# Last stage of a decoder block: the first of seven block products is placed one step forward, and the newest MLP tile's transpose is issued on ScalarE's DMA queue

## The chip, the cores and the metric

The kernel runs on one core of one Trainium2 chip. The metric is device time in microseconds of that core for one execution, as the median of repeated runs. Before the change it is 1565.66 us over three runs (1565.0, 1565.66 and 1566.17).

## The reference

One layer (`DEPTH = 1`) for 256 tokens of width 2048, all in float32. Ahead of the part that matters here come a norm, one wide projection, a sparse attention and a retention branch, their gated sum and a projection `w_out` that is added to `x`. What the change touches is the end of the MLP:

```python
h2 = rms_norm(x, ln2_g[l])
x = x + jnp.square(jax.nn.relu(h2 @ w_ff1[l])) @ w_ff2[l]     # w_ff1 2048 x 8192, w_ff2 8192 x 2048
```

The output is (1, 256, 2048) float32.

## The kernel before

**Products.** A float32 product is made of three TensorE (PE) matmuls. Weights and activations are each split into a rounded part `hi` and a rest `lo`, and `products` (L477 to L479) adds act-hi with weight-hi, act-hi with weight-lo and act-lo with weight-hi into one PSUM bank. ScalarE (ACT) writes a weight tile's `whi` at L427, VectorE (DVE) writes its `wlo` at L429, for 128x1024 elements at a time, from a `raw` tile that SyncE (SP) loads at L382 (1 MB each). `weights(item)` hands out such a pair; it also starts the loads and splits of the items that follow in the list `use`.

**The MLP.** The 8192 hidden columns go in eight groups of 1024 (g = 0 to 7). A group's hidden values are made with tokens on the partitions, as tiles of 128 tokens x 512 columns, named by token half t and column half i. For the second matmul each tile is turned by `turn_in`: ACT gathers the two 16-bit halves of every word into `halves` (L519), a DMA transposes that into the tile itself (L523, 256 KB, on SP's queue), ACT puts the words together again (L528), and `split_into` splits them into `act` hi (ACT, L501) and lo (DVE, L502). L519 writes what the DMA reads, and L528 waits for it to land. In the last group (LAST = 7) the two tiles of i = 1 come first, then (t 0, i 0), and (t 1, i 0) is the newest: its `halves` is the last L519 of the program.

**The last stage.** `ending` multiplies the last group's hidden values with its 1024 rows of `w_ff2`. Its order is written by hand in `ESTEPS`. A step (i, h, s) stands for column block i (512 columns) and two of the eight row tiles, half h and pair s within it; it takes both token halves, so 2 x 2 x 3 = 12 matmuls of 128x512 (in block 3, token half 1 is done in two pieces of 256 columns). For blocks 1 and 2 only the half h = 0 is done so. Their half h = 1 is done by the seven products of a 2 x 2 block scheme: a number n in `ESTEPS` is product n, of 6 matmuls, and `ETILES` and `PRODUCTS` say which weight tile (A to D) and which form of the activations it takes. Products 0 and, later, others use `act` as it is; four forms are differences of quarters of `act` (`fm`, made in `end_forms`, L1470 and L1474 on DVE, split at L506 on ACT and L507 on DVE). Weight tiles are added in place at L413 between products (A + B when step (0, 0, 1) is reached, and so on, by `ESUMS`).

Product 0 takes weight tile A and the form X11, the quarter of `act` with token half 0 and the first two row tiles of half 1, that is hidden tile (t 0, i 1). Step (0, 0, 0) takes row tiles of half 0 in both token halves, that is the hidden tiles (t 0, i 0) and (t 1, i 0).

**What else stands there.** The partial sums of the earlier groups are in DRAM (`sums`); GpSimd (POOL) adds to them by DMA (L1460) what ACT scales at L1459. `stream(i)` reads block i back into `room` (L1494, on SP's queue; block 0 at step (3, 1, 0), block 2 at product 0). ACT copies products 0, 1 and 3 out of PSUM at L1532; DVE combines them (L1534, L1537, L1538), adds them to `room` (L1498), and ACT issues the output DMAs (L1501).

**What sets the order.** Each engine runs its own instructions in a fixed order. `step()` advances every generator in `work` by one `yield`, once an item, so moving an item also moves what the generators and `weights` emit around it. A wait on ACT, on DVE or in SP's queue holds everything behind it on that engine.

Of the kernel before, what the change touches and what calls it, by code (L numbers as in the profile page):

```python
# [13 lines left out]
U16 = mybir.dt.uint16  # L14
# [4 lines left out]
P = 128  # L19
# [110 lines left out]
def merged(g):  # L130

    f = iter([("F2", g - 1, i, h, s) for i, h in F2_COLS for s in range(KC // HC)])
    out = []
    for n, p in enumerate(ORDER):
        for h in range(HK // KC):
            out += [("Q", g, n, h, s) for s in range(KC // HC)]
            out.append(next(f))
        if p == 4:
            out.append(next(f))
    return out + list(f)  # L140
# [9 lines left out]
OTHERS = [(("O", i), h) for i in range(3) for h in range(DK // KC)]  # L150
LAST = NG - 1
ETILES = {"A": (1, 0), "B": (2, 0), "C": (2, 1), "D": (1, 1)}
ESTEPS = ((0, 1, 0), (0, 1, 1), (3, 1, 0), (3, 1, 1), (0, 0, 0), 0, (0, 0, 1), 1, (1, 0, 0), 2, (1, 0, 1), 3, 4, (2, 0, 0), 5, (2, 0, 1), 6,
          (3, 0, 0), (3, 0, 1))
BEHIND = {0: (2, 1), 2: (1, 0), 1: (2, 0), 3: (3, 0)}
STREAMS = {(3, 1, 0): 0, (1, 0, 0): 1, (2, 0, 0): 3}
# [23 lines left out]
def block_kernel(ctx, tc, cst, rot, xt, gains, w, x, ret_gn_g, ret_gn_b, out):  # L180
    nc = tc.nc
# [29 lines left out]
    W_NORM, W_SOFT, W_GN, W_CROSS, W_ROWS, W_LAST, W_QUERY, W_PROBS, W_INDEX = 3, 5, 7, 8, 7, 6, 5, 5, 5  # L211
# [4 lines left out]
    def nm(s):  # L216
        uid[0] += 1
        return f"{s}_{uid[0]}"
# [6 lines left out]
    def mid(shape, dtype=F32):  # L225
        return late["ep"].tile(list(shape), dtype, tag="mid", name=nm("mid"), bufs=n_mid[late["ep"].name])
# [66 lines left out]
    for g in range(1, NG):  # L293
        use += merged(g)
    use += [("F2", LAST) + z if type(z) is tuple else ("E", z, ETILES[PRODUCTS[ORDER[z]][1]][1]) for z in ESTEPS]

# [199 lines left out]
    def split_into(act, k0, nk, t, ps):  # L496

        src = ps.rearrange("p (c i) -> p c i", c=nk)
        hi = act[0][:, k0:k0 + nk, t * P:(t + 1) * P]
        lo = act[1][:, k0:k0 + nk, t * P:(t + 1) * P]  # L500
        nc.scalar.activation(hi, src, AF.Copy)  # L501
        nc.vector.tensor_tensor(lo, src, hi.bitcast(F32), op=ALU.subtract)  # L502
# [6 lines left out]
    def interleaved(a):  # L509
        return a.bitcast(U16).rearrange("p (j h) -> p h j", h=2)  # L510

    def planes(a):
        return a.bitcast(U16).rearrange("p (h j) -> p h j", h=2)

    def turned(src, halves, wait, tied=False, dst=None, mirror=None, gap=1):

        mirror = src if mirror is None else mirror
        with tc.issue_after(late["split"]) if tied else nullcontext():
            nc.scalar.activation(planes(halves), interleaved(src), AF.Copy)  # L519
        for _ in range(gap):  # L520
            yield
        with tc.issue_after(late["loaded"]) if gap > 1 else nullcontext():
            nc.sync.dma_start_transpose(mirror.bitcast(U16).rearrange("p (c r) -> p c r", r=P), halves.bitcast(U16))  # L523
        for _ in range(wait):
            yield
        with tc.issue_after(late["split"]):
            if dst is None or len(dst.shape) == 2:
                nc.scalar.activation(interleaved(halves if dst is None else dst), planes(mirror), AF.Copy)  # L528
            else:
                nc.scalar.activation(dst.bitcast(U16).rearrange("p c (i h) -> p h c i", h=2), planes(mirror).rearrange("p h (c i) -> p h c i", i=P), AF.Copy)  # L530

    def turn_in(act, k0, t, src, tile_for, wait, land=W_CROSS, tied=False, mirror=None, gap=1):

        for _ in range(wait):
            yield
        halves = tile_for((P, BN))
        yield from turned(src, halves, land, tied, mirror=mirror, gap=gap)
        split_into(act, k0, 4, t, halves)

    hT = act_pair(0)  # L540
# [86 lines left out]
    def key_tile(t, a):  # L627

        for _ in range(2 * t):
            yield  # L630
        halves = ep.tile([P, BN], F32, tag="halves", name=nm("halves"), bufs=2)
        yield from turned(a, halves, W_CROSS + 2)
        nc.scalar.activation(kT[:, :, t * P:(t + 1) * P], halves.rearrange("p (h i) -> p h i", h=4), AF.Copy, scale=gqk)
# [6 lines left out]
    def index_tile(t, half):  # L640

        for _ in range(t if half else 4 + 2 * t):
            yield
        if "iqT" not in late:
            late["ik2"] = mid([P, T, 2, ID])
            late["iqT"] = ep.tile([P, IH // 2, S], F32, tag="a1", name="iqT")
        c = IH // 4
        dst = late["iqT"][:, half * c:(half + 1) * c, t * P:(t + 1) * P]
        yield from turned(iqs[:, t, half * BN:(half + 1) * BN], stage(), W_INDEX + t if half else W_CROSS, dst=dst)
        turned_iq.add((t, half))  # L650
# [159 lines left out]
    for j in range(NKV):  # L810
        ps = run_block(("AQ", j), of(hT))
        r = cp.tile([P, GRP * T], F32, name=nm("r"))
# [198 lines left out]
    for gate, u in ((z, u) for z in BESIDE for u in range(2)):  # L1011
# [10 lines left out]
        for item in beside(gate, u):  # L1022
# [10 lines left out]
            else:  # L1033
                branch(item, of(oT if gate == "GA" else hT))
                i = item[0][1] - 2 * u
# [57 lines left out]
    def normed(j, ys, gb, sg):  # L1093
        mv, vr, nb = small(4 * T), small(2 * T), small(2 * T)
        for t in range(T):
            for a in range(2):
                st = small(6)
                nc.vector.bn_stats(st, ys[t][:, a * RV:(a + 1) * RV])
                nc.vector.bn_aggr(mv[:, 4 * t + 2 * a:4 * t + 2 * a + 2], st)
        mean, var = (mv.rearrange("p (a b) -> p a b", b=2)[:, :, i] for i in range(2))  # L1100
        nc.vector.tensor_copy(vr, var)
        yield
        r = rsqrt(vr, 2 * T, 1.0)
        nc.vector.scalar_tensor_tensor(nb, mean, -1.0, r, op0=ALU.mult, op1=ALU.mult)
        yield
        for t in range(T):
            y = ys[t]
            for a in range(2):
                c = slice(a * RV, (a + 1) * RV)
                i = 2 * t + a  # L1110
                nc.scalar.activation(y[:, c], y[:, c], AF.Identity, scale=r[:, i:i + 1], bias=nb[:, i:i + 1])
            nc.vector.tensor_tensor(y, y, gb[0], op=ALU.mult)
            nc.vector.tensor_tensor(y, y, gb[1], op=ALU.add)
            yield
            nc.vector.tensor_tensor(y, y, sg[t], op=ALU.mult)
            work.append(turn_in(rT, 4 * j, t, y, halves, *((W_GN - 1 + t,) if j < 2 else (W_GN - 3 + t, 5))))

    for j in range(4):
        if j < 2:

            i = j
# [5 lines left out]
        for src in (ret_gn_g, ret_gn_b):  # L1127
            g = mid([P, BN])
# [71 lines left out]
    for i in range(4):  # L1200
        ms = mss[i] if i in pair else gates(i)
        ps = run_block(("UR", i), of(rT), ps=pair.get(i), k0=PARTS[-1][0] * KC if i in pair else 0)
        for t, m in enumerate(ms):
            g = sgb[:, t, i * BN:(i + 1) * BN]
            nc.vector.tensor_tensor(g, ps[t], g, op=ALU.mult)
            nc.vector.tensor_tensor(m, m, g, op=ALU.add)
            if i < 2:
                work.append(turn_whole(i, t, m))
            elif i < 3:
                work.append(turn_in(mT, 4 * i, t, m, mid, 2 + 2 * t))  # L1210
            else:
                tails.append(turn_in(mT, 4 * i, t, m, kept, 0, 11, mirror=kept((P, BN)), gap=6))
                next(tails[-1])
# [184 lines left out]
    def put(*new):  # L1398
        for (t, i), z, src in new:
            ys[t, i] = squared(z, src)  # L1400
        for (t, i), _, _ in new:
            hidden(g, t, i)
# [4 lines left out]
    def hidden(g, t, i):  # L1407
        act, y = [z[:, g % 2 * FG:] for z in hid[:2]], ys.pop((t, i))
        wait, room, land = (1 + 2 * t, spread if g or not i else stage, 7 if g or i else 4 + t)
        if g and not i:  # L1410
            wait, land = {NG - 1: ((3, 4), (0, 2))}.get(g, ((4, 9), (1, 8)))[t]
        turn = turn_in(act, 4 * i, t, y, room, wait, land, g > 0)
        work.append(marked(turn, t) if (g, i) == (LAST, 1) else turn)

    def marked(turn, t):
        yield from turn
        inner.append(t)
# [8 lines left out]
    for i, part in F1_PARTS:  # L1426
        up[i] = run_block(("F1", i), lambda k, t: form(blocks[k // HK][t], k % HK), ps=up.get(i),
                          k0=part[0] * KC, k1=(part[-1] + 1) * KC)
        if part[-1] < DK // KC - 1:
            continue  # L1430
        for t in range(T):
            ys[t, i] = squared(stage(), up[i][t])
            if i:
                hidden(0, t, i)
# [145 lines left out]
    for t in range(T):  # L1580
        hidden(0, t, 0)
# [43 lines left out]
```

## Time and profile before

| | |
|---|---|
| median of 3 runs | 1565.66 us (1565.0 to 1566.17) |
| the profiled execution's own time | 1565.19 us |
| its span, first to last instruction | 1563.4 us |
| time around the span | 1.79 us |
| DVE busy | 1353.4 us (87%) |
| ACT busy | 1154.2 us (74%) |
| POOL busy | 93.1 us (6%) |
| mean granted TensorE clock | 1.000 |
| DMA moved | 373.21 MB, mean 239 GB/s |

Times are microseconds from the start of the span, unless marked ns. A row of the timeline gives start, duration, engine, line and operation, output and input, and in brackets how long the engine stood idle before it and what released it. PEld is TensorE's weight load, which runs beside its matmuls; "SPq" and "ACTq" are DMA instructions that the engine issues. "Us to landing" is the time from a DMA's issue until its data is there.

### The profile page before, as it was taken

Reading aid. Unit: us, or ns where it says so; the run is one execution under the profiler, and the core shown is the slowest. Engines: PE = TensorE matmul, PEld = TensorE weight load, DVE = VectorE, ACT = ScalarE, POOL = GpSimd, SP = SyncE. Lnnn points to the kernel's source line nnn. Section 1 sums busy time; section 2 is a strip of 40 time slices with the busy share of each in tenths; the row PEclk is TensorE's granted clock in tenths of the full one; section 3 lists DMA queues with packets and bytes.
Section 4 is the critical chain, followed back from the end, with each engine's and each line's share of the span. In section 5 each row is a group of like instructions: output and inputs, shape, how many; then the busy total and the mean of one; then the engine's idle time right before and its main releaser. Section 6 shows DMA issues by size and latency. Waiting matters only on the chain.

```text
span 1563.4 us, 19344 instructions
## 1 busy us (share of the span) xinstructions
PE 1557.7 (100%) x7094; PEld 1298.8 (83%) x7094; DVE 1353.4 (87%) x1526; ACT 1154.2 (74%) x1372; POOL 93.1 (6%) x139
## 2 busy tenths in 40 slices
PE   9999999999999999999999999999999999999999
PEld 8988888888888888888888888888888888888887
DVE  6678889899999898688678889998989899999987
ACT  7767887776666666477676888787878787878784
POOL 0000000000000001302000000101010000000000
PEclk9999999999999999999999999999999999999999
DMA  9956658866565755969769785979789787979675
GB/s 335 238 188 190 198 171 267 282 213 242 212 242 210 267 187 189 335 207 291 237 204 350 205 281 182 276 226 280 231 263 237 247 249 242 270 241 250 231 191 191
DMA packets 154959, 373.21 MB, mean 239 GB/s; under 512 B 93504, under 2 KB 100288, under 8 KB 119536
## 3 DMA queue, kind: packets, MB, share of 16 engines
q1 hardware_dynamic: 137728, 332.30, 64.4%
q0 software_dynamic: 14400, 35.33, 9.7%
q10 hardware_dynamic: 2736, 4.34, 0.8%
q8 instruction: 55, 0.90, 0.2%
q14 instruction: 40, 0.33, 0.1%
HBM read 323.44 MB, written 27.26 MB: 224 GB/s over the span
## 4 chain that ended last, share of the span: by engine, by line
PE 99%; DMA 0%; DVE 0%; SPq 0%; ACT 0%; issue 0%
PE pm L478 12%; PE pm L477 12%; PE pm L479 12%; PE pf L477 11%; PE pf L479 11%; PE pf L478 11%; PE pq L477 9%; PE pq L479 9%; PE pq L478 9%; PE pa L478 1%; PE pa L477 1%; PE pa L479 1%; DMA raw<-in_w_dram 0%; PE pa L1065 0%; PE pt L797 0%; PE pa L769 0%
## 5 line engine op out<-in xcount | busy, mean ns | idle before, releaser
L429 DVE TENSOR_TENSOR wlo<-raw,whi 128x1024 fp32r<-128x1024 f32 (+2 forms) x535 | 632.5, 1201 | 121.8 <-ACT whi L427 116.2
L427 ACT ACTIVATE whi<-raw 128x1024 fp32r<-128x1024 f32 (+2 forms) x534 | 549.0, 1039 | 244.6 <-PE pm L479 82.5
L477 PE MATMUL pm<-whi,act 128*128 128x512 f32 (+1 forms) x748 | 287.0, 384 | 0.8 <-ACT act L547 0.7
L478 PE MATMUL pf<-wlo,act 128*128 128x512 f32 x740 | 287.0, 388 | 0.0
L479 PE MATMUL pf<-whi,act 128*128 128x512 f32 x740 | 287.0, 388 | 0.0
L477 PE MATMUL pf<-whi,act 128*128 128x512 f32 x740 | 286.8, 388 | 0.0
L478 PE MATMUL pm<-wlo,act 128*128 128x512 f32 (+1 forms) x748 | 285.8, 382 | 0.2 <-DVE wlo L429 0.2
L479 PE MATMUL pm<-whi,act 128*128 128x512 f32 (+1 forms) x748 | 285.9, 382 | 0.0
L429 DVE TENSOR_TENSOR wlo<-rawc,whi 128x1024 fp32r<-128x1024 f32 x176 | 215.2, 1222 | 38.1 <-ACT whi L427 36.4
L427 ACT ACTIVATE whi<-rawc 128x1024 fp32r<-128x1024 f32 x176 | 185.9, 1057 | 59.9 <-PE pf L479 26.1
L413 DVE TENSOR_TENSOR raw<-raw,raw 128x2048 f32<-128x2048 f32 (+1 forms) x92 | 207.1, 2252 | 0.2
L477 PEld LDWEIGHTS pf<-whi,act 128*128 128x128 f32 x740 | 138.9, 188 | 28.7 <-DVE room L1537 0.3
L479 PEld LDWEIGHTS pf<-whi,act 128*128 128x128 f32 x740 | 138.9, 188 | 28.6
L478 PEld LDWEIGHTS pf<-wlo,act 128*128 128x128 f32 x740 | 138.9, 188 | 28.6
L477 PEld LDWEIGHTS pm<-whi,act 128*128 128x128 f32 x748 | 140.5, 188 | 26.6 <-ACT act L547 0.9
L479 PEld LDWEIGHTS pm<-whi,act 128*128 128x128 f32 x748 | 140.4, 188 | 25.7 <-DVE act L548 0.2
L478 PEld LDWEIGHTS pm<-wlo,act 128*128 128x128 f32 x748 | 140.4, 188 | 25.1 <-DVE wlo L429 0.5
L478 PE MATMUL pq<-wlo,xf 128*128 128x512 f32 x392 | 152.5, 389 | 0.0
L479 PE MATMUL pq<-whi,xf 128*128 128x512 f32 x392 | 152.5, 389 | 0.0
L477 PE MATMUL pq<-whi,xf 128*128 128x512 f32 x392 | 152.5, 389 | 0.0
L1460 POOL DMA_DIRECT2D sums<-halves x56 | 48.3, 974 | 658.6 <-ACT halves L1459 658.6
L479 PEld LDWEIGHTS pq<-whi,xf 128*128 128x128 f32 x392 | 73.6, 188 | 15.3
(270 smaller groups left out, 1805.8 us busy)
## 6 DMA issues: line engine op xcount, KB each, us to landing
raw<-in_w_dram SPq DMA_DIRECT2D x181, 1024.0 KB, 6.1
rawc<-in_w_dram SPq DMA_DIRECT2D x88, 1024.0 KB, 5.7
sums<-halves POOLq DMA_DIRECT2D x56, 256.0 KB, 8.5
spare<-in_w_dram SPq DMA_DIRECT2D x7, 1024.0 KB, 10.4
raw<-in_w_dram SPq DMA_DIRECT2D x8, 736.0 KB, 8.2
raw<-in_w_dram SPq DMA_DIRECT2D x7, 512.0 KB, 7.3
raw<-in_w_dram SPq DMA_DIRECT2D x8, 368.0 KB, 7.3
stg<-in_x_dram SPq DMA_DIRECT2D x8, 256.0 KB, 7.5
```

The lines of the kernel that those rows point to most:

```text
L413: nc.vector.tensor_tensor(one, one, two, op=ALU.add)
L427: late["split"] = nc.scalar.activation(a, src, AF.Copy).ins
L429: lows.append(nc.vector.tensor_tensor(b, src, a.bitcast(F32), op=ALU.subtract).ins)
L477: nc.tensor.matmul(d, h, hi, start=first, stop=False, skip_group_check=skip)
L478: nc.tensor.matmul(d, h, lo, start=False, stop=False, skip_group_check=skip)
L479: nc.tensor.matmul(d, l, hi, start=False, stop=last, skip_group_check=skip)
L1460: nc.gpsimd.dma_start(sums[:, t, i * BN:(i + 1) * BN], z, accum_op=ALU.add)
```

## The change

Two things. In `ESTEPS`, product 0 changes places with step (0, 0, 0), which it followed. And the transpose of hidden tile (t 1, i 0) of the last group is issued by ACT instead of SP.

```diff
-ESTEPS = ((0, 1, 0), (0, 1, 1), (3, 1, 0), (3, 1, 1), (0, 0, 0), 0, (0, 0, 1), 1, (1, 0, 0), 2, (1, 0, 1), 3, 4, (2, 0, 0), 5, (2, 0, 1), 6,
+ESTEPS = ((0, 1, 0), (0, 1, 1), (3, 1, 0), (3, 1, 1), 0, (0, 0, 0), (0, 0, 1), 1, (1, 0, 0), 2, (1, 0, 1), 3, 4, (2, 0, 0), 5, (2, 0, 1), 6,
           (3, 0, 0), (3, 0, 1))
...
-    def turned(src, halves, wait, tied=False, dst=None, mirror=None, gap=1):
+    def turned(src, halves, wait, tied=False, dst=None, mirror=None, gap=1, queue=nc.sync):
...
-            nc.sync.dma_start_transpose(mirror.bitcast(U16).rearrange("p (c r) -> p c r", r=P), halves.bitcast(U16))
+            queue.dma_start_transpose(mirror.bitcast(U16).rearrange("p (c r) -> p c r", r=P), halves.bitcast(U16))
...
-        turn = turn_in(act, 4 * i, t, y, room, wait, land, g > 0)
+        turn = turn_in(act, 4 * i, t, y, room, wait, land, g > 0, queue=nc.scalar if (g, i, t) == (LAST, 0, 1) else nc.sync)
```

`turn_in` passes `queue` on to `turned`. The instructions of the program are the same up to this place, and their number on TensorE is the same. Tile numbers are given in the order in which tiles are made, so a number can stand for another tile after the change: `whi_12679` and `raw_12575` belong to step (0, 0, 0) before and to product 0 after; `whi_12700` and `raw_12591` the other way round.

On ACT, behind the last L519 of the program, this is the start of the difference, with the semaphores that a row waits for (DMAHW3 counts the transpose of tile (t 0, i 0), `halves_12561`; DMAHW5 that of the newest tile, `halves_12612`; Activation is ACT's own):

```order
 L519 ACTIVATE halves_12612<-stg_12398 128x1024 [waits DMASW4_49,Activation_49]
 L1459 ACTIVATE halves_12643<-pf_12517,q_7743 128x512 [waits PE_49]
+L523 DMA_TRANSPOSE stg_12398<-halves_12612 128x8x128 [waits DMAHW3_49,Activation_49]
 L1459 ACTIVATE halves_12646<-pf_12518,q_7743 128x512 [waits DVE_49,PE_49]
 L427 ACTIVATE whi_12658<-raw_12542 128x1024
-L528 ACTIVATE halves_12561<-stg_12063 128x2x512 [waits DMAHW3_49]
+L528 ACTIVATE halves_12561<-stg_12063 128x2x512
+L427 ACTIVATE whi_12679<-raw_12575 128x1024 [waits DMAHW1_49,PE_49]
+L501 ACTIVATE act_7742<-halves_12561 128x4x128 [waits Activation_49]
+L528 ACTIVATE halves_12612<-stg_12398 128x2x512 [waits DMAHW5_49]
+L427 ACTIVATE whi_12700<-raw_12591 128x1024 [waits DMAHW2_49,DVE_49,PE_49]
```

The transpose now stands between the two L1459 and waits for the transpose ahead of it to land. Three of the four L506 (`fm`), which stood before the newest tile's L528, stand behind it, and the weights of product 0 are split ahead of it.

On DVE, at the same place in the program, from the split of step (3, 1, 1)'s weights (`wlo_12659`) on:

```order
 L429 TENSOR_TENSOR wlo_12659<-raw_12542,whi_12658 128x1024
+L429 TENSOR_TENSOR wlo_12680<-raw_12575,whi_12679 128x1024
+L502 TENSOR_TENSOR act_7742<-halves_12561,act_7742 128x4x128
+L429 TENSOR_TENSOR wlo_12701<-raw_12591,whi_12700 128x1024
+L502 TENSOR_TENSOR act_7742<-halves_12612,act_7742 128x4x128
+L507 TENSOR_TENSOR fm<-room,fm 128x256
+L413 TENSOR_TENSOR raw_12575<-raw_12575,raw_12610 128x1024
+L1474 TENSOR_TENSOR room<-room 128x256
+L429 TENSOR_TENSOR wlo_12732<-raw_12591,whi_12731 128x1024
 L507 TENSOR_TENSOR fm<-room,fm 128x256
 L1474 TENSOR_TENSOR room<-room 128x256
```

The two L502 and the two weight splits come first; all four L507 and the last two L1474 now stand behind the newest tile's L502, where before only one L507 did. DVE has as many of each as before.

On SP, from the transpose of tile (t 0, i 0) on (`raw_12610` is weight tile B, `raw_12662` that of block 1's half h = 0):

```order
 L523 DMA_TRANSPOSE stg_12063<-halves_12561 128x8x128
 L382 DMA raw_12610<-in_w_dram 128x2048
-L523 DMA_TRANSPOSE stg_12398<-halves_12612 128x8x128
+L1494 DMA room<-sums 128x512 x2
 L382 DMA raw_12662<-in_w_dram 128x2048
-L1494 DMA room<-sums 128x512 x4
-L382 DMA raw_12775<-in_w_dram 128x2048
+L1494 DMA room<-sums 128x512 x2
+L382 DMA raw_12774<-in_w_dram 128x2048
```

The transpose is gone from SP, and block 0's two reads of `sums` stand ahead of the load of `raw_12662` instead of behind it. POOL's order is the same.

More of the change, by code (lines that the diff above doesn't have):

```diff
@@ L530, in turned, with turn_in @@
                 nc.scalar.activation(dst.bitcast(U16).rearrange("p c (i h) -> p h c i", h=2), planes(mirror).rearrange("p h (c i) -> p h c i", i=P), AF.Copy)
-    def turn_in(act, k0, t, src, tile_for, wait, land=W_CROSS, tied=False, mirror=None, gap=1):
+    def turn_in(act, k0, t, src, tile_for, wait, land=W_CROSS, tied=False, mirror=None, gap=1, queue=nc.sync):
         for _ in range(wait):
@@ L536, in turn_in @@
         halves = tile_for((P, BN))
-        yield from turned(src, halves, land, tied, mirror=mirror, gap=gap)
+        yield from turned(src, halves, land, tied, mirror=mirror, gap=gap, queue=queue)
         split_into(act, k0, 4, t, halves)
```

## The prediction

> **What bounds the kernel now.** I read the page's busy shares first, then TensorE's waits over the whole run, then the last 50 us engine by engine, because the order of the instructions differs only there.
>
> ```profile
> span 1563.4 us, 19344 instructions
> PE 1557.7 (100%) x7094; PEld 1298.8 (83%) x7094; DVE 1353.4 (87%) x1526; ACT 1154.2 (74%) x1372; POOL 93.1 (6%) x139
> PE 99%; DMA 0%; DVE 0%; SPq 0%; ACT 0%; issue 0%
> PE pa L269 <- DVE warm L266: 1.1, 1, 1.1
> PE pm L477 <- ACT act L547: 0.7, 1, 0.7
> PE pm L478 <- DVE wlo L429: 0.2, 1, 0.2
> ```
>
> TensorE makes up 99% of the chain of waits, and its recorded waits are 2.0 us in all, each on a line of the first stage (the warm-up, then bank pm). So in the last stage a change can save only what the weight loads' waits and the spacing of matmuls still hide. These rows show it, from the timeline of matmuls, the weight loads' waits from 1520 us on and their timeline:
>
> ```profile
> 1479.72 0.39 PE L479 MATMUL pq<-whi,xf 128*128 128x512 f32 x1
> ...
> 1523.24 0.39 PE L479 MATMUL pf<-whi,act 128*128 128x512 f32 x1
> 1527.72 0.40 PE L477 MATMUL pf<-whi,act 128*128 128x512 f32 x1
> 1556.66 0.28 PE L477 MATMUL pf<-whi,act 128*128 128x256 f32 x1
> PEld pf L477 <- ACT room L1532: 0.2, 1, 0.2
> 1548.38 0.19 PEld L477 LDWEIGHTS pf<-whi,act 128*128 128x128 f32 x1 [0.28 <-DVE room L1537]
> ```
>
> Step (0, 0, 0) begins at 1527.72. From there to 1556.66 stand 126 matmuls of 512 columns (six steps of 12, seven products of 6, and 12 of block 3). The 193 such rows from 1479.72 to 1523.24 stand (1523.24 - 1479.72) / 192 = 0.2267 us apart; at that spacing the 126 need 28.56 us, and they took 28.94. **All that TensorE loses behind the place of the change is about 0.4 us**, 0.02% of the run. That is the whole prize, and what is named in it lies at L1532 and L1537, some 17 to 20 us further on.
>
> **The swap itself.** It adds and removes no matmul. Product 0 needs hidden tile (t 0, i 1), which is two tiles older; step (0, 0, 0) needs the newest. Did it wait for it?
>
> ```profile
> 1524.12 1.38 ACT L528 ACTIVATE halves<-stg 128x1024 uint16<-128x1024 uint16 x1 [1.58 <-DMA stg<-halves]
> 1525.37 1.03 ACT L427 ACTIVATE whi<-raw 128x1024 fp32r<-128x1024 f32 x1
> 1526.30 0.61 ACT L501 ACTIVATE act<-halves 128x512 fp32r<-128x512 f32 x1
> 1526.82 0.40 ACT L506 ACTIVATE fm<-room 128x256 fp32r<-128x256 f32 x1
> 1526.43 1.23 DVE L429 TENSOR_TENSOR wlo<-raw,whi 128x1024 fp32r<-128x1024 f32 x1 [2.31 <-ACT whi L427]
> 1527.57 0.68 DVE L502 TENSOR_TENSOR act<-halves,act 128x512 fp32r<-128x512 f32 x1
> 1528.88 0.39 PE L479 MATMUL pf<-whi,act 128*128 128x512 f32 x1
> ```
>
> ACT idled 1.58 us for the transpose and DVE 2.31 behind it, but the tile was ready at 1528.25 and its lo part first used at 1528.88: 0.6 us to spare. So a wait of ACT and DVE goes that TensorE never felt. The swap moves that use by 6 x 0.2267 = 1.36 us, which adds margin and saves **nothing**; if the cover were gone (a tile late by over 0.6 us), it would save up to 1.36.
>
> **The transpose on ACT.** What it does on SP, and what stands around it on ACT:
>
> ```profile
> 1516.06 0.33 SPq L382 DMA_DIRECT2D raw<-in_w_dram  x1
> 1516.86 1.23 SPq L523 DMA_TRANSPOSE stg<-halves  x1
> stg<-halves SPq DMA_TRANSPOSE x1, 7.2
> 1515.79 1.05 ACT L519 ACTIVATE halves<-stg 128x1024 uint16<-128x1024 uint16 x1
> 1516.73 1.25 ACT L1459 ACTIVATE halves<-pf,q 128x512 f32<-128x512 f32 x2
> 1517.87 1.06 ACT L427 ACTIVATE whi<-raw 128x1024 fp32r<-128x1024 f32 x1
> 1518.82 1.38 ACT L528 ACTIVATE halves<-stg 128x1024 uint16<-128x1024 uint16 x1
> ```
>
> On SP it was issued 0.02 us after L519 ended (1516.84), so it starts no sooner on ACT. No row shows ACT issuing a transpose. Bounds from rows:
>
> ```profile
> L523 SPq DMA_TRANSPOSE stg<-halves x46: 1231/1236/4347, 54.0 to 1516.9; - x46
> DMA to landing us min/median/max: 3.0/5.5/11.5
> sums<-x ACTq DMA_DIRECT2D x8, 256.0 KB, 2.3
> stg<-halves SPq DMA_TRANSPOSE x1, 5.2
> ```
>
> ACT is held for 1.23 us (the shortest and the median, and this very transpose) up to 4.35; I take 1.23. Landing lies between 2.3 us (256 KB issued by ACT) and 11.5 (the slowest transpose); I take 5.2, the transpose just ahead, issued at 1509.34.
>
> Then ACT goes on as follows, each step by the start-to-start distance of its kind in the rows above. Transpose 1516.85 to 1518.08; second L1459 at 1518.08 instead of 1517.30; `whi` of (3, 1, 1) at 1518.65 (+0.78); L528 of the older tile 1519.60; `whi` of product 0 1520.85; L501 1521.80; **L528 of the newest tile from 1522.32**, if it has landed: by 5.2 us it lands at 1522.05. `whi` of (0, 0, 0) 1523.57; L501 1524.50. On DVE, `wlo` of product 0 runs 1521.92 to 1523.14 and is needed at 1527.72 + 0.23; `wlo` of (0, 0, 0) ends at 1525.8, needed at 1529.3; L502 of the newest tile ends at 1526.4, needed at 1530.2. All early by over 3 us.
>
> What is late next is what moved behind them: DVE's `fm` work. A row of two gives the distance from start to start: 0.34 us for 128x256 elements, 1.13 for 128x1024.
>
> ```profile
> 1518.97 1.23 DVE L429 TENSOR_TENSOR wlo<-raw,whi 128x1024 fp32r<-128x1024 f32 x1 [0.28 <-ACT whi L427]
> 1523.36 0.76 DVE L507 TENSOR_TENSOR fm<-room,fm 128x256 fp32r<-128x256 f32 x2
> 1531.91 1.22 DVE L413 TENSOR_TENSOR raw<-raw 128x1024 f32<-128x1024 f32 x1
> 1533.05 2.35 DVE L429 TENSOR_TENSOR wlo<-raw,whi 128x1024 fp32r<-128x1024 f32 x2
> 1544.11 1.23 DVE L429 TENSOR_TENSOR wlo<-raw,whi 128x1024 fp32r<-128x1024 f32 x1 [0.44 <-ACT whi L427]
> ```
>
> After L502 come four L507 and two L1474 (6 x 0.34), the sum A + B and two `wlo` (3 x 1.13): 5.43 us from 1526.35, so the next sum at L413 starts at 1531.8. Before, it started at 1531.91: the same within 0.1 us. From there to 1543.67 DVE has no pause, then 0.44 us, and then TensorE waits for its L1537. So if DVE is late by L at 1531.9, the end is late by **max(0, L - 0.44)**. Here L = -0.1, so 0; being early gains nothing either, as that pause waits for ACT, which waits for TensorE.
>
> The other queues: SP loses a transpose of 1.23 us, and its two reads of block 0 go ahead of the load of `raw_12662`, which waits for DVE's `wlo` of (3, 1, 1). That one, at 1518.97 before, starts when its `whi` is done, 0.78 us later, and ends at 1520.98.
>
> ```profile
> raw<-in_w_dram SPq DMA_DIRECT2D x1, 1024.0 KB, 8.4
> sums<-halves POOLq DMA_DIRECT2D x56, 256.0 KB, 8.5
> 1539.44 0.86 SPq L1494 DMA_DIRECT2D room<-sums  x2
> ```
>
> At its 8.4 us the load lands at 1529.4. Its reader on ACT stands behind the fourth L506 and an L1532; that L506 waits for DVE's last L1474 (done at about 1530.0 in the count above), so the reader comes near 1530.9, 1.5 us after the landing. POOL's last sum follows the second L1459, which ends at 1518.8; at 8.5 us it lands at 1527.3 and is read back at 1539.44, hidden.
>
> **Sum:** 0 (swap) + 0 (ACT held 1.23 us, hidden by its old wait of 1.58) + 0 (DVE) = 1565.19 us on the profiled execution's scale. That execution lies 0.47 us under the median of the three runs, so on the median's scale I predict 1565.7 us.
>
> **Rivals.** The measurement tells about 0.2% from no change, here 3.1 us.
>
> *It lands no sooner (15%).* On SP a 1 MB load, issued 0.8 us ahead in the same queue, may have cost it 2 us; on ACT's queue nothing is ahead of it. If the 7.2 us stay, it lands at 1524.05, L528 and all behind it slip by 1.73 us, L is 1.63, and the end moves by +1.2: 1566.9. For it: the same engines carry both. Against: ACT's own 256 KB DMAs landed in 2.3 us among loads. The Trainium skill speaks for this rival (DMA: Bandwidth & Descriptors, "Issuing engines are not separate DMA queues"): DMAs of all issuers interleave on the same 16 engines, and a second issuer saves only sequencer time; by that the landing stays 7.2.
>
> *ACT is held longer by the issue (4%).* At 4.35 us ACT's work slips by 3.12 against the count above, L is 3.0, the end +2.6: 1568.3. For: SP's reads of block 0 are issued at the same time. Against: the median of 46 is the 1.23 us that I take.
>
> *Slower: ACT's queue stands behind the landing (5%).* ACT runs in order, and behind the newest tile's L528 stand the weights of (0, 0, 0) and (0, 0, 1) and all later `fm`. Each us of landing past 1522.32 is a us of L. The end is 3.1 us late from L = 3.54 on, a landing of 9.1 us; at 11.5 L is 5.9 and the end +5.5: 1571.2. For: such landings occur in this trace. Against: the two nearest took 5.2 and 7.2. ACT's transpose also waits for the one on SP: that landed at 1509.34 + 5.2 = 1514.5, 2.3 us before it is asked for, but at 11.5 us it would hold ACT until 1520.84, for +3.5; this is a part of the 5%. The Trainium skill demands that wait (same page, "Silent corruption: two transposing streams in flight at once"): the later stream must wait for the earlier one's full completion. The instruction order shows the wait, and by the 5.2 us row it costs nothing.
>
> *Faster (5%).* The different order of DVE's rows at L1498 happens to remove the waits at 1545 and 1548: at most -0.4, 1565.3. Over 0.2% faster would need 3.1 us where TensorE loses 0.4: 1%.
>
> That the change does nothing it says isn't likely: the instruction order shows both moves; it only has no wait of TensorE to remove.
>
> **How the numbers follow.** Forecast (within 0.3 us of 1565.7) 70%, the rivals 15, 4, 5, 5, other 1%. The range runs from 1565.0 (lowest run) - 0.4 = 1564.6 to 1565.7 + 2.6 = 1568.3, which takes in the landing of 7.2 and the longest issue and leaves out the late landing. Slower by over 0.2%: 5%; faster: 1%; within: 94%.
>
> **What would show it.** Right: a transpose of about 1.23 us on ACT at 1516.9; L528 of the newest tile near 1522.3 with no DMA wait; product 0 on TensorE at 1527.7 and step (0, 0, 0) at 1529.1 without idling; the sum at L413 near 1531.8; the wait at L1537 still 0.28. Wrong: a wait of L528 past 1523, a longer issue, or TensorE's weight loads waiting for `wlo` or L1537 by more than 0.3; or a time that differs by over 1 us with no such row, for then the loss lay where these rows show none.

## The result, and the profile after

The changed kernel took **1577.34 us** (median of 6 runs, 1575.0 to 1578.98) against 1565.98 us (6 runs, 1565.0 to 1566.81) for the kernel before: a ratio of **1.0071, interval 1.006 to 1.0082**. It is slower, where no change was forecast, and 9 us beyond the upper end of the range. The profiled execution took 1576.82 us.

The page of the changed kernel first: its span, the busy time of each engine, and the shares of the chain that ended last.

```profile
span 1575.0 us, 19342 instructions
PE 1562.2 (99%) x7094; PEld 1302.0 (83%) x7094; DVE 1352.7 (86%) x1526; ACT 1153.8 (73%) x1372; POOL 93.1 (6%) x139
PE 95%; ACT 2%; DMA 2%; DVE 1%; issue 1%; ACTq 0%
```

The span grew by 11.6 us and TensorE's busy time by only 4.5. The chain, 99% TensorE before, now passes through ACT and a DMA. TensorE's waits over the whole run (engine, bank and line, what it waited for: us in all, times, longest) name the place.

```profile
PE pf L477 <- ACT whi L427: 6.5, 1, 6.5
PE pa L269 <- DVE warm L266: 1.1, 1, 1.1
PE pt L670 <- DVE mid L663: 0.6, 1, 0.6
PE pa L681 <- DVE mid L671: 0.5, 1, 0.5
PE pf L478 <- DVE wlo L429: 0.5, 1, 0.5
```

One wait of 6.5 us on bank pf is new, with a short one behind it. The two at L670 and L681 lie in an early stage that the change doesn't touch; they stand in the traces of some kernels (e1 and e4, below) and not of others (e2 and e7). Just ahead of them the changed kernel is 0.3 us early (its first matmul of 512 columns there at 76.73 against 77.05), and behind them 1.0 late (L681 at 83.88 against 82.87): the older tile's transpose was issued at 1510.36 instead of 1509.34. So of the 11.6 us, **1.0 lies ahead of the change and 10.6 behind it**.

ACT's own timeline shows why TensorE waited (start, duration, engine, line, what it writes and reads; in brackets the idle time ahead and what ended it).

```profile
1516.81 1.04 ACT L519 ACTIVATE halves<-stg 128x1024 uint16<-128x1024 uint16 x1
1517.87 1.50 ACTq L523 DMA_TRANSPOSE stg<-halves  x1
1519.48 0.69 ACT L1459 ACTIVATE halves<-pf,q 128x512 f32<-128x512 f32 x1 [1.06 <-DVE room L1474]
1521.01 1.36 ACT L528 ACTIVATE halves<-stg 128x1024 uint16<-128x1024 uint16 x1
1522.24 1.03 ACT L427 ACTIVATE whi<-raw 128x1024 fp32r<-128x1024 f32 x1
1523.17 0.62 ACT L501 ACTIVATE act<-halves 128x512 fp32r<-128x512 f32 x1
1534.47 1.34 ACT L528 ACTIVATE halves<-stg 128x1024 uint16<-128x1024 uint16 x1 [10.68 <-DMA stg<-halves]
1535.69 1.03 ACT L427 ACTIVATE whi<-raw 128x1024 fp32r<-128x1024 f32 x1
```

The issue took 1.50 us. The 1.06 us of idle time behind it carry DVE's name, but they end 0.11 us after the issue does: it is the issue that held ACT. The newest tile's L528 then waited **10.68 us** for the transpose. The next row is the `whi` that TensorE waited for. What was issued between 1517 and 1519 us, with the size and the time from issue to landing:

```profile
raw<-in_w_dram SPq DMA_DIRECT2D x1, 1024.0 KB, 5.7
room<-sums SPq DMA_DIRECT2D x2, 256.0 KB, 7.1
sums<-halves POOLq DMA_DIRECT2D x1, 256.0 KB, 10.4
stg<-halves ACTq DMA_TRANSPOSE x1, 16.6
```

**The transpose took 16.6 us to land**, against 7.2 on SP's queue. On DVE the work behind it stands as follows.

```profile
1536.75 1.22 DVE L429 TENSOR_TENSOR wlo<-raw,whi 128x1024 fp32r<-128x1024 f32 x1 [11.61 <-ACT whi L427]
...
1538.49 0.42 DVE L507 TENSOR_TENSOR fm<-room,fm 128x256 fp32r<-128x256 f32 x1
...
1543.91 1.22 DVE L413 TENSOR_TENSOR raw<-raw 128x1024 f32<-128x1024 f32 x1
```

From the first L507 to the sum at L413 lie 5.42 us. That sum, at 1531.91 before, is 12.0 us later, 11.0 without the 1.0 ahead of the change. From 1536.75 to 1567.9 DVE has no pause. Last, stretches of the changed kernel, for TensorE (stretch, its length, busy time and instructions, granted clock, DMA share, GB/s):

```profile
1530.00:1533.00 3.00, 0.29 (x2) 0.99 1.06 225
1533.00:1536.70 3.70, 0.00 (x0) 0.50 0.08 22
1536.70:1543.10 6.40, 5.87 (x13) 0.50 0.08 13
1543.10:1571.00 27.90, 27.90 (x131) 1.00 0.49 176
```

After the wait the granted clock was 0.50 for some 6.3 us. At the 0.2267 us of the prediction 13 matmuls take 2.95 us; they took 6.40, so this stretch lost 3.4 us more: 0.5 in the short wait for `wlo`, some 2.9 by the half clock. From the last matmul ahead of the wait (1529.90) to the first at full speed behind it (1543.27) lie 14 distances of 0.2267 in 13.37 us: **TensorE by itself lost 10.2 us**. The clock fell at about 1533.0, 2.7 us after the last matmul had ended (1530.29), and came back at about 1543.2, 6.4 us after the next had begun: 10.2 us at half. The Trainium skill (TensorE: Matmul & The Clock Gate, Part 1) says that the clock halves after an idle window of about 3.4 us and comes back after a busy one, and that the windows run freely. The trace agrees in so far as 10.2 us is three such windows, by an estimate from the page's 3.4; counted from the last matmul or from the next one, neither the 2.7 nor the 6.4 us is one window.

### The profile page after: what moved, and what is told of

The parts are those of the page before. It is cut to its first block, busy times and chain, and to the rows that moved or that the text cites. A ratio compares the mean times of both kernels' runs of the same rounds, so it can differ in the third digit from the quotient of the medians.

```text
span 1575.0 us, 19342 instructions
## 1 busy us (share of the span) xinstructions
PE 1562.2 (99%) x7094; PEld 1302.0 (83%) x7094; DVE 1352.7 (86%) x1526; ACT 1153.8 (73%) x1372; POOL 93.1 (6%) x139
## 4 chain that ended last, share of the span: by engine, by line
PE 95%; ACT 2%; DMA 2%; DVE 1%; issue 1%; ACTq 0%
PE pm L477 11%; PE pm L478 11%; PE pm L479 11%; PE pf L478 10%; PE pf L479 10%; PE pf L477 10%; PE pq L478 9%; PE pq L479 9%; PE pq L477 9%; DMA stg<-halves 1%; PE pa L477 1%; PE pa L478 1%; PE pa L479 1%; ACT whi L427 1%; DVE wlo L429 1%
## 5 line engine op out<-in xcount | busy, mean ns | idle before, releaser
L427 ACT ACTIVATE whi<-rawc 128x1024 fp32r<-128x1024 f32 x176 | 185.9, 1056 | 62.2 <-PE pf L479 26.1
L413 DVE TENSOR_TENSOR raw<-raw,raw 128x2048 f32<-128x2048 f32 (+1 forms) x92 | 206.8, 2248 | 0.2
L478 PEld LDWEIGHTS pq<-wlo,xf 128*128 128x128 f32 x392 | 73.6, 188 | 15.6
```

Of the source, the lines that this page charges most:

```text
L413: nc.vector.tensor_tensor(one, one, two, op=ALU.add)
L427: late["split"] = nc.scalar.activation(a, src, AF.Copy).ins
L478: nc.tensor.matmul(d, h, lo, start=False, stop=False, skip_group_check=skip)
```

## The experiments

Four questions: which half of the change costs the time; why the transpose lands so late (in the expectations, T is that it shares the 16 engines with what SP and POOL have under way, and T2 its later form); whether DVE's chain (D) or TensorE's restart at half clock (P) then sets the end; and whether the loss can be taken away. In the diffs, - is the changed kernel and + the experiment. Each ratio is against the kernel before, run on the same chip.

### One half of the change at a time

`e1_swap_only` has the new order of steps, with all transposes on SP:

```diff
-        turn = turn_in(act, 4 * i, t, y, room, wait, land, g > 0, queue=nc.scalar if (g, i, t) == (LAST, 0, 1) else nc.sync)
+        turn = turn_in(act, 4 * i, t, y, room, wait, land, g > 0)
```

> Only the swap of product 0 and step (0, 0, 0); the newest tile's transpose stays on SyncE's queue. Theory T (the loss is the late landing of the transpose on ScalarE's queue): landing near 7 us as before, no wait of TensorE for whi, time within 1 us of the kernel before (1565 to 1567). Rival R1 (the loss comes from the swap and what it reorders): most of the 11 us stays, 1572 or more.

Measured: 1565.93 us against 1565.76, ratio 1.0001 (0.9992 to 1.001). TensorE had no wait in the last stage. The swap is worth nothing, as forecast.

`e2_act_only` has the transpose on ACT and the old order:

```diff
-ESTEPS = (..., (3, 1, 1), 0, (0, 0, 0), (0, 0, 1), ...
+ESTEPS = (..., (3, 1, 1), (0, 0, 0), 0, (0, 0, 1), ...
```

> Only the transpose on ScalarE's queue; product 0 stands behind step (0, 0, 0) as before. T: the transpose lands some 16 us after its issue, ScalarE idles about 10 us at L528, the time is 1575 to 1579. R1: landing 7 us or less, the time is 1565 to 1568.

Measured: 1576.95 us, ratio 1.0072 (1.0055 to 1.0089). From ACT's timeline of this kernel:

```profile
1517.13 1.50 ACTq L523 DMA_TRANSPOSE stg<-halves  x1
...
1532.70 1.34 ACT L528 ACTIVATE halves<-stg 128x1024 uint16<-128x1024 uint16 x1 [9.66 <-DMA stg<-halves]
```

The transpose landed 15.5 us after its issue. **The move to ACT's queue makes up the whole loss**, with the order on SP that it brings (two of the reads of `sums` ahead of the load).

### Is ACT's queue slow by itself?

`e3_older_on_act` puts the older tile's transpose on ACT, one tile earlier, and leaves the newest on SP:

```diff
-... queue=nc.scalar if (g, i, t) == (LAST, 0, 1) else nc.sync)
+... queue=nc.scalar if (g, i, t) == (LAST, 0, 0) else nc.sync)
```

> As the changed kernel, but the older tile's (t 0, i 0) transpose is on ScalarE's queue, 7 us earlier, where SyncE's queue carries one load and GpSimd's no sum; the newest is back on SyncE. T (what counts is the packets of other queues beside it): it lands 5 to 9 us after its issue, costs nothing, 1565 to 1568. Rival R2 (a transpose issued by ScalarE takes some 16 us whatever runs beside it): it lands near 16 us, ScalarE idles at L528 until about 1527, 1569 to 1572.

Measured: 1565.85 us, ratio 1.0 (0.9991 to 1.001). The DMAs of this kernel issued from 1505 to 1520 us:

```profile
stg<-halves ACTq DMA_TRANSPOSE x1, 5.2
stg<-halves SPq DMA_TRANSPOSE x1, 5.7
```

So the queue is not slow. What differs is the moment: two of POOL's sums and SP's load of block 1 are issued soon after the newest tile's transpose (at 1518.7, 1520.5 and 1522.4 us in the changed kernel).

### Which neighbour?

`e4_sp_held` puts a 4 KB DMA on SP that reads the transposed tile, so that SP's load of block 1 and three of its four reads of `sums` start only after the landing (in the changed kernel two reads go ahead of it, here one):

```diff
+            if queue is nc.scalar:
+                nc.sync.dma_start(probe, mirror.bitcast(U16)[:, :16])
...
+    probe = dp.tile([P, 16], U16, name="probe")
```

> As the changed kernel, but SyncE's queue is held until the newest transpose has landed, by a small DMA that reads the transposed tile: load B and one read of sums stand ahead of it, the load of block 1 and three reads of sums behind. T: with little beside it the transpose lands 5 to 9 us after its issue; the load behind it comes some 3 us later than in the kernel before, so the time is 1566 to 1570. R2: landing 16 us as in the changed kernel, and the loads come behind it, 1577 or more.

Measured: 1569.82 us, ratio 1.0025 (1.0016 to 1.0034). The transpose landed in **9.4 us**, just over the 5 to 9 expected, still beside POOL's sums. Packets of each DMA queue from 1522 to 1526 us (packets, MB, share of the 16 engines; q10 holds ACT's transpose, q1 SP's DMAs, q0 POOL's sums):

```profile
q0 software_dynamic: 183, 0.34, 64.8%
q10 hardware_dynamic: 1024, 0.26, 36.1%
q1 hardware_dynamic: 115, 0.20, 22.9%
```

`e6_no_last_sum` is the other side, without POOL's last two sums and with SP's queue as in the changed kernel. It leaves a part out: column block 3 of its output lacks one group.

```diff
-                nc.gpsimd.dma_start(sums[:, t, i * BN:(i + 1) * BN], z, accum_op=ALU.add)
+                if (g, i) != (LAST - 1, D // BN - 1):
+                    nc.gpsimd.dma_start(sums[:, t, i * BN:(i + 1) * BN], z, accum_op=ALU.add)
```

> As the changed kernel, but GpSimd's last two sums (column block 3 of the group before the last, 2 x 256 KB) are left out, so that column block is short of one group; ScalarE still scales them. T (the transpose's small packets take turns with those of the other queues and end only when nearly all that is queued beside them is through): without that queue's 0.5 MB the transpose lands 2 to 4 us sooner, 12.5 to 14.5 us after its issue, and the time falls by as much, to 1573.5 to 1575.5. R2 (a transpose issued by ScalarE is slow by itself): landing stays at 16 us, the time at 1576 to 1578.

Measured: 1567.1 us, ratio 1.0012 (1.0002 to 1.0021); the transpose landed in **7.2 us**, far sooner than I had expected. The same view of this kernel from 1522 to 1524 us, and then of the changed kernel from 1524 to 1526:

```profile
q10 hardware_dynamic: 1052, 0.26, 100.7%
q1 hardware_dynamic: 79, 0.22, 27.5%
```

```profile
q0 software_dynamic: 148, 0.28, 78.3%
q10 hardware_dynamic: 312, 0.08, 26.7%
q1 hardware_dynamic: 31, 0.04, 6.6%
```

A 256 KB transpose is 1056 packets, nearly all of 256 bytes. Without the sums 1052 of them passed within 2 us; beside the sums 312 did. How far the sums hold it back varies: in e4, from 1524 to 1526 us, 660 passed beside 132 packets of the sums. So with the sums, but without the load and the second read of block 0, it takes 9.4 us (e4); with the load and both reads, but without the sums, 7.2 (e6), for there it is nearly through when the load's packets begin (15 packets on q1 from 1523 to 1524 us, the landing at 1524.47). **With all of them it is 16.6**: beside the sums the transpose isn't through when the load of block 1 begins, and then it has a third queue to share with. The second read of block 0 has a part in it too: from 1523 to 1524 us the changed kernel passed 110 packets of SP's reads and 98 of the transpose. The changed kernel from 1527 to 1529 us and from 1529 to 1531:

```profile
q1 hardware_dynamic: 53, 0.43, 54.4%
q0 software_dynamic: 54, 0.11, 30.9%
q10 hardware_dynamic: 53, 0.01, 4.5%
```

```profile
q1 hardware_dynamic: 181, 0.62, 90.1%
q10 hardware_dynamic: 181, 0.05, 12.5%
q0 software_dynamic: 30, 0.03, 9.2%
```

53 packets against 53, 181 against 181: **one packet of the transpose for one of SP's queue**, and in the first stretch 54 of the sums' beside them. In that stretch a packet of SP's (0.43 MB / 53 = 8 KB) takes 0.544 x 16 x 2 us / 53 = 0.33 us of an engine, one of the sums' 0.309 x 16 x 2 / 54 = 0.18, and one of the transpose 0.027. A transpose packet that shares in turns with both there costs 0.54 us instead of 0.027. The Trainium skill has the rule (DMA: Bandwidth & Descriptors, "Queues, rings and completion order"): each DMA engine goes round the queue rows that have work, packet by packet. These counts agree with it; whether the page's packet, which holds several descriptors, is the one that the profile counts, no run here shows.

`e5_small_packets` tests this with smaller packets: the load of block 1 as four DMAs of 256 KB, with rows of 2 KB.

```diff
-                one = nc.sync.dma_start(r[:, :, :n], src).ins
+                for c in [slice(j, j + 1) for j in range(KC)] if key[0] == ("F2", LAST, 1, 0) else [slice(0, KC)]:
+                    one = nc.sync.dma_start(r[:, c, :n], src[:, c]).ins
```

> As the changed kernel, but the load of block 1's weights, which follows on SyncE's queue, is issued as four loads of 256 KB, with rows of 2 KB instead of 8 KB. Theory T2 (GpSimd's sums slow the transpose's packets until this load is under way, and from then on they get one 256-byte packet for each packet of the load): smaller neighbours mean more turns in the same time, the transpose lands 13 to 15.5 us after its issue and the time falls by 1 to 3.5 us. Rival B (the engines share by bytes, or GpSimd's sums alone set the landing): landing 16 us or more, the time within 0.8 us of the changed kernel.

Measured: 1573.89 us, ratio 1.0054 (1.0037 to 1.0071), and a landing of 14.3 us. The queues from 1526.5 to 1528.5 us:

```profile
q0 software_dynamic: 73, 0.14, 66.2%
q1 hardware_dynamic: 97, 0.19, 40.8%
q10 hardware_dynamic: 98, 0.03, 10.6%
```

97 against 98: the turns stay and pass faster, at 98 packets in 2 us instead of 53. The landing came 2.3 us sooner, inside what was expected. By the landing and the time alone this would be weak: with the load in one piece the landing lay between 15.5 and 17.7 us in three kernels, and this ratio's interval overlaps the changed kernel's. The counts are what carries it. The sums were still there, and so was most of the loss.

### What sets the end once the transpose is late

`e7_fm_first` places the newest tile's L528 one item later, so that ACT and DVE split the weights of step (0, 0, 0) and do a part of the `fm` work (two L506, two L507 and one L1474) ahead of the wait:

```diff
-            wait, land = {NG - 1: ((3, 4), (0, 2))}.get(g, ((4, 9), (1, 8)))[t]
+            wait, land = {NG - 1: ((3, 4), (0, 3))}.get(g, ((4, 9), (1, 8)))[t]
```

> As the changed kernel, but the newest tile's L528 is put one item later: the split of step (0, 0, 0)'s weights, two of the four fm splits on ScalarE and VectorE and one difference stand ahead of the wait instead of behind it. The landing should stay at 16 us. Theory D (after the wait VectorE's chain of work sets the end, as in the prediction's formula): the next sum at L413 comes 2.5 us sooner after the landing and the time falls by 2 to 3 us, to 1574 to 1575.5. Rival P (TensorE's own late start and its lower clock after the wait set the end): within 0.6 us of the changed kernel, 1576.5 to 1578.

Measured: 1575.02 us, ratio 1.0055 (1.0038 to 1.0072). ACT's and DVE's timeline, then TensorE's stretch behind its wait of 6.7 us:

```profile
1534.39 1.34 ACT L528 ACTIVATE halves<-stg 128x1024 uint16<-128x1024 uint16 x1 [10.17 <-DMA stg<-halves]
...
1541.44 1.22 DVE L413 TENSOR_TENSOR raw<-raw 128x1024 f32<-128x1024 f32 x1
...
1553.72 1.22 DVE L429 TENSOR_TENSOR wlo<-raw,whi 128x1024 fp32r<-128x1024 f32 x1 [0.41 <-ACT whi L427]
```

```profile
1536.40:1543.00 6.60, 6.56 (x17) 0.54 0.33 102
```

L528 starts at 1534.39 (1534.47 in the changed kernel), and the sum at L413 follows after 7.05 us instead of 9.44. The median is 2.3 us lower, but the two ratios' intervals overlap, so the time alone does not settle the question. DVE's pauses do. Here DVE still pauses 0.41 us for ACT at 1553.72, as it did for 0.44 us in the kernel before: it has time to spare, so TensorE's late start and half clock set the end, at a loss of 9.7 us (15 distances of 0.2267 in the 13.14 us from 1529.38 to 1542.52). In the changed kernel that pause is gone: there DVE's chain sets the end, and TensorE's own 10.2 us lie just below it. So both D and P hold, each in one kernel, and they are a few tenths of a us apart.

### Can the loss be taken away?

`e8_pool_held` puts a 4 KB DMA on POOL's queue that reads the transposed tile, and has the last two sums issued behind it:

```diff
+            if queue is nc.scalar:
+                late["probe"] = nc.gpsimd.dma_start(probe, mirror.bitcast(U16)[:, :16]).ins
...
-                nc.gpsimd.dma_start(sums[:, t, i * BN:(i + 1) * BN], z, accum_op=ALU.add)
+                with tc.issue_after(late["probe"]) if (g, i) == (LAST - 1, D // BN - 1) else nullcontext():
+                    nc.gpsimd.dma_start(sums[:, t, i * BN:(i + 1) * BN], z, accum_op=ALU.add)
```

> As the changed kernel, with the whole computation, but GpSimd's last two sums are held until the newest transpose has landed, by a small DMA on GpSimd's queue that reads the transposed tile. T2: landing near 7 us as without the sums, the time 1566.3 to 1567.8. Rival (what helped without the sums was their bytes or the missing work, not when they run): landing over 10 us, the time over 1569.

Measured: 1567.02 us against 1565.85, ratio 1.0008 (0.9999 to 1.0017); the transpose landed in 7.3 us. `e9_pool_held_fm_first` is e8 with e7's line, `(0, 3)`, as well:

> Both: GpSimd's last two sums held until the landing, and the newest tile's L528 one item later, so that weights and fm work stand ahead of the wait. T2 with the prediction's formula: landing near 7 us, VectorE is not late, the time is that of the kernel before within 0.6 us, 1565.4 to 1566.6, and not faster, because TensorE has no wait left to lose.

Measured: 1565.86 us, ratio 0.9999 (0.999 to 1.0009), with the same landing of 7.3 us. The sum at L413 in e8, then in e9, and TensorE's weight loads' waits in e9 from 1500 us on:

```profile
1535.17 1.21 DVE L413 TENSOR_TENSOR raw<-raw 128x1024 f32<-128x1024 f32 x1
```

```profile
1531.45 1.22 DVE L413 TENSOR_TENSOR raw<-raw 128x1024 f32<-128x1024 f32 x1
```

```profile
PEld pf L477 <- DVE room L1541: 0.2, 1, 0.2
PEld pf L477 <- ACT room L1536: 0.2, 1, 0.2
```

The loss is gone, and what is left of TensorE's waits is what the kernel before had. No version beat the kernel before: it has no more than the 0.4 us to give that the prediction counted.

### All runs by one formula

The prediction gave the end as late by max(0, L - 0.44), with L the lateness of the sum at L413 against 1531.91. Here it is for each profiled execution, with the shift ahead of the change (the older tile's issue less 1509.34) taken off both sides. In e3, where ACT issues that transpose, the shift is taken from SP's load ahead of it (1507.59 less 1506.98). Times are in us; "lost" is the span less 1563.4 and less the shift. TensorE's own loss is counted as above, where it has a wait of over 1 us in the last stage.

| kernel | newest transpose's landing | older issue | sum at L413 | L | L - 0.44, not below 0 | TensorE's own loss | lost |
|---|---|---|---|---|---|---|---|
| changed | 16.6 | 1510.36 | 1543.91 | 10.98 | 10.5 | 10.2 | 10.6 |
| e2 | 15.5 | 1509.61 | 1542.14 | 9.96 | 9.5 | 9.8 | 9.9 |
| e5 | 14.3 | 1510.22 | 1541.47 | 8.68 | 8.2 | 6.9 | 8.1 |
| e7 | 17.7 | 1509.16 | 1541.44 | 9.71 | 9.3 | 9.7 | 9.9 |
| e4 | 9.4 | 1510.70 | 1537.07 | 3.80 | 3.4 | none | 3.4 |
| e8 | 7.3 | 1510.82 | 1535.17 | 1.78 | 1.3 | none | 1.4 |
| e6 | 7.2 | 1509.75 | 1533.95 | 1.63 | 1.2 | none | 1.3 |
| e1 | 7.6 (on SP) | 1511.54 | 1534.50 | 0.39 | 0 | none | 0.0 |
| e3 | 5.7 (on SP) | 1509.95 (on ACT) | 1531.52 | -1.00 | 0 | none | 0.0 |
| e9 | 7.3 | 1509.37 | 1531.45 | -0.49 | 0 | none | 0.1 |

It holds within 0.1 us in eight of ten. In e4, e6 and e8 TensorE has no wait of over 1 us in the last stage and its clock stays at 1.00, so no restart can account for their loss: there DVE's chain behind L528 sets the end, without a pause from the first split behind the wait (1529.91 in e4) on. In e2 and e7, 0.4 and 0.6 us over the formula, TensorE's own loss is the larger of the two, and DVE's pause for ACT is there again (0.34 and 0.41 us): there TensorE's restart sets the end. The larger of the two losses gives the measured one within 0.2 us in all ten.

## Why the prediction was wrong

- **The swap, 0 us: right.** e1 measured it by itself.
- **ACT held by the issue: right in kind, 0.3 us too little.** 1.23 us was taken from SP's row; on ACT it was 1.50 here and 1.33 to 1.64 in the experiments. The work behind it ran in the forecast order: the earlier L528 was forecast at 1519.60 and stood at 1521.01 - 1.02 = 1519.99.
- **The step that failed: "Landing lies between 2.3 us (256 KB issued by ACT) and 11.5 (the slowest transpose); I take 5.2".** It was 16.6, and 15.5, 14.3 and 17.7 in three experiments that keep both neighbours. Both ends were rows of other conditions: the upper one a transpose in SP's queue, the lower one a plain ACT DMA. I chose by size and by the nearest transpose, and did not ask what else would be under way in those microseconds. "On ACT's queue nothing is ahead of it" was the error: nothing ahead in the queue, but on the engines two sums, two reads and a load beside it.
- **The rival "ACT's queue stands behind the landing" was the right mechanism, at 5%.** It had the place (L528, with the weights and `fm` work behind it), the point from which it decides (9.1 us) and a price per microsecond. Its price ended at 11.5 us and +5.5. With the measured landing its own rule gives L = 1516.85 + 16.6 - 1522.32 - 0.1 = 11.0 and an end later by 11.0 - 0.44 = 10.6 us, which is what was lost behind the change.
- **The rival "it lands no sooner" was priced rightly too.** e6 and e8 have its 7.2 and 7.3 us: +1.2 forecast, +1.1 and +1.2 measured; the intervals reach from about 0 to 3 us, so that closeness is partly luck, but the traces' own 1.3 and 1.4 bear it out. The rule of the Trainium skill that spoke for it (DMA: Bandwidth & Descriptors, "Issuing engines are not separate DMA queues": the issuers' DMAs interleave, and only issue time is saved) is borne out by the packet counts as to the interleaving. That a second issuer changes nothing else is not: the same transpose took 7.2 us in one queue and 16.6 in the other.
- **DVE's `fm` work as the next late thing: right.** 5.43 us were counted to the sum at L413, and 5.42 measured.
- **Not foreseen: the half clock behind TensorE's wait.** It took some 2.9 us. With the waits TensorE lost 10.2 us, just less than the 10.5 of DVE's chain, so it added nothing to the end here; in e2 and e7 TensorE's loss was the larger and set the end.
- **The chances.** 94% for no change rested on the landing alone, for which no row of the trace had the same conditions.

## What to carry to other kernels

Before a DMA is moved to another queue, list what the other queues have under way from its issue to its landing, with their packet sizes: here it was served in a run in its old queue, and took turns with them in the new one. With packets of 256 bytes beside packets of 8 KB that cost it 9.4 us (7.2 to 16.6), and an in-order engine that waits for it passes the delay on to all that stands behind. If it must be there, hold the neighbours that can wait (e8: 16.6 to 7.3 us), and put work that doesn't need it ahead of the wait (e9).

## What the hardware showed that I had not expected

- The same 1056 packets passed in 2 us when nothing but SP's DMAs was beside them (e6), and in over 11 us beside sums and loads (the changed kernel: the first 9 from 1521 to 1523 us, the landing at 1534.47).

- In the kernel before, SP's queue carried the transpose past a sum all the same, though the sum's first packets came at about 1521.0; its queues from 1520 to 1522 us:

```profile
q1 hardware_dynamic: 1042, 0.40, 81.7%
q0 software_dynamic: 37, 0.08, 76.2%
```

- 1042 packets of SP's queue against 37 of POOL's is no turn for turn, nor is it from 1521.0 to 1521.5 alone (515 against 8). Why the sums held back the transpose in ACT's queue (312 against 148 in the changed kernel, 660 against 132 in e4) and not in SP's stays open.
- ACT's transpose was issued at 1517.87, and its first packets show between 1521 and 1523 us, when SP's 1 MB load ahead, issued at 1517.06 and landed 5.7 us later, was about through. Why it began no sooner, by turns with that load, stays open too.
- TensorE's clock stayed at half for 10.2 us in the changed kernel (1533.0 to 1543.2), as in e2 and e7, and for 3.4 us in e5 (about 1535.2 to 1538.6), where the wait was 4.2 us and the clock fell only after TensorE had started again at 1534.33.
